# Prompt attention: the value products of a pair of heads side by side, block of keys by block, in a bank of their own

## The chip, the cores and the metric

The kernel runs on one core of one Trainium2 chip. The metric is the device time of one execution in microseconds (us). Engines: PE is TensorE (matrix products and transposes), DVE is VectorE, ACT is ScalarE, POOL is GpSimd (here mostly an issuer of DMAs), SP is SyncE (issues the weight loads). Every engine works through its own instructions in the order in which the built program has them, and waits on semaphores for the others.

## The reference, cut to what matters

One step of a decoder layer for a prompt of 512 tokens and 8 samples of 4 tokens. The part that is changed is the prompt's dilated attention: 12 heads of 64 columns, softmax over the keys allowed by three dilations, then the product with the values.

```python
HEAD_DIM = 64
DIL_HEADS = 12
DIL_PAIRS = ((128, 1), (512, 4), (2048, 16))
...
    s = jnp.einsum('bthd,btnhd->bthn', q, kg, preferred_element_type=jnp.float32) * (HEAD_DIM ** -0.5)
    s = jnp.where(valid[None, :, None, :], s, -jnp.inf)
    m = jnp.max(s, axis=-1, keepdims=True)
    p = jnp.exp(s - m)
    den = jnp.sum(p, axis=-1, keepdims=True)
    num = jnp.einsum('bthn,btnhd->bthd', p, vg.astype(jnp.float32))
```

Around it in the same layer: one input projection (for queries, keys, values, gates), a gated linear attention, an output projection, a convolutional feed-forward block and norms. The samples' attention over a cache of 1024 positions is computed beside the prompt's.

## The kernel before

Activations lie feature-major: 128 features on the partitions, 512 prompt and 32 sample tokens along the free axis. All big products are made in tiles of 128 output features (`in_tile`, L225): 16 blocks of input features, three products of split operands, two halves of 272 columns, so 96 matmuls to a tile, into one of two PSUM buffers `g`. A tile's result is taken out by DVE or ACT (`rope`, `scaled`, `gates`) into one of a few SBUF buffers, and only then is its PSUM buffer free for the tile after next.

The attention stage starts after six query tiles. For each of six pairs of heads it makes a key tile and a value tile, transposes the values (L584), and calls `prompt_attention`. That takes four blocks of 128 queries (`qi`), n = 128, 256, 384 and 512 keys, and in each the two heads (`e`): scores on PE (L548), bias and row maximum on DVE (L551, L553), exponential and row sum on ACT (L554), reciprocal on DVE (L555), scaling on ACT (L556), transposes of the probabilities on PE (L558), copy out of PSUM on ACT (L559), products with the values on PE (L561), copy of the result on ACT (L563). Scores, transposes and value products of one head and block share one PSUM tile `s`; there are three of these (`sps`), also used by the short transposes L382 and L584. A head's probabilities `t` come from five buffers (`ttile`). A value product has 128 rows and 64 columns of the array: head 0 writes partitions 0 to 63, head 1 partitions 64 to 127. Products of float32 operands show up in the trace as two instructions each (240 for the 120 of L561), transposes as one.

In the same stage run the samples' scores (`sample_scores`, DVE, with its loads issued by POOL) and, twice, `sample_mix`: softmax of the samples' scores (DVE L454 to L460, ACT L450, L464, L465, small PE transposes L444, L477, L484, L489) and their value products (L507), with cache blocks `kv` loaded by POOL (L395, L396) into four buffers that are freed by the products of the group before.

The order on each engine is found at build time by a scheduler that plays the program through on a timeline of its own; a tile's buffer is taken when its turn in the program's order of allocations comes. Weight loads and splits run ahead under a high priority. Two gates matter below. The evacuation of a projection tile needs a free SBUF buffer, which a pair of heads holds until its last scores are computed. And the gate tiles that come after the last pair need space which opens only when all prompt attention is done (`gates(DP)`, DVE L533).

Of the kernel before, what the change touches and what calls it, by code (L numbers as in the profile page):

```python
# [12 lines left out]
AF = mybir.ActivationFunctionType  # L13
# [4 lines left out]
P = 128  # L18
# [105 lines left out]
def _build(tc, nc, es, xT, st_gla, ck, cv, conv_in, vecs, w_in, w_gu, w_out, w_up, w_dn,  # L124
# [112 lines left out]
    def ttile(name, dt=F32):  # L237
        return PA.tile([P, NT], dt, tag="T", name=name, bufs=5)
# [61 lines left out]
    def sps():  # L300
        return pS.tile([P, 512], F32, tag="s", name="s")
# [4 lines left out]
    def in_tile(c0, units=None):  # L306
        ps = gps()
        gemm(ps, units or [wunit(w_in, ks, c0) for ks in H8], xg)
        return ps[:, :, :HT]
# [29 lines left out]
    for k in range(KD):  # L339
        for s in range(2):  # L340
            nc.tensor.matmul(psz[s][:2 * RANK, :HT], wz[:, k, :], xg[k][0][:, s * HT:(s + 1) * HT],
                             start=(k == 0), stop=False, skip_group_check=True)
            nc.tensor.matmul(psz[s][:RANK, :HT], wz[:, k, :RANK], xg[k][1][:, s * HT:(s + 1) * HT],
                             start=False, stop=(k == KD - 1), skip_group_check=True)
# [22 lines left out]
    def scaled(ps, name, mul=None):  # L367
        with evac():
            out = etile(name)
            if mul is None:  # L370
                nc.vector.tensor_mul(hv(out), ps, hv(rstd))
            else:
                nc.vector.scalar_tensor_tensor(hv(out), ps, mul, hv(rstd), op0=OP.mult, op1=OP.mult)
        return out
# [10 lines left out]
    o = [None] * KD  # L385
# [153 lines left out]
    def prompt_attention(p, q, k, vt):  # L539
        for e in range(2):  # L540
            r = slice(64 * e, 64 * e + 64)
            nc.scalar.activation(qz[r, e, :], q[r, :TP], AF.Copy)
        for qi in range(4):
            n = (qi + 1) * P
            for e in range(2):
                r = slice(64 * e, 64 * e + 64)
                psc = sps()
                nc.tensor.matmul(psc[:, :n], qz[:, e, qi * P:(qi + 1) * P], k[:, :n], start=True, stop=True)  # L548
                t = ttile("t")
                st = PA.tile([P, 4], F32, tag="st", name="st", bufs=6)  # L550
                nc.vector.tensor_tensor_reduce(t[:, :n], psc[:, :n], bp[:, (3 - qi) * P:], 0.125, -3e38,  # L551
                                               OP.add, OP.max, st[:, 0:1])
                nc.vector.tensor_scalar(st[:, 1:2], st[:, 0:1], -1.0, None, op0=OP.mult)  # L553
                nc.scalar.activation(t[:, :n], t[:, :n], AF.Exp, bias=st[:, 1:2], accum_out=st[:, 2:3])  # L554
                nc.vector.reciprocal(st[:, 3:4], st[:, 2:3])  # L555
                nc.scalar.activation(t[:, :n], t[:, :n], AF.Copy, scale=st[:, 3:4])  # L556
                for j in range(qi + 1):
                    nc.tensor.transpose(psc[:, j * P:(j + 1) * P], t[:, j * P:(j + 1) * P], ident)  # L558
                nc.scalar.activation(t[:, :n], psc[:, :n], AF.Copy)  # L559
                for j in range(qi + 1):  # L560
                    nc.tensor.matmul(psc[r, :P], vt[:, j * P + 64 * e:j * P + 64 * e + 64], t[:, j * P:(j + 1) * P],  # L561
                                     start=(j == 0), stop=(j == qi))
                nc.scalar.activation(o[10 + p][r, qi * P:(qi + 1) * P], psc[r, :P], AF.Copy)  # L563

    for p in range(DP):
        o[10 + p] = rowsA.tile([P, NT], F32, tag="R", name="ob")
# [8 lines left out]
    for p in range(DP):  # L575
        kT = rope(in_tile(C_KB + p * P), etile("rp"))
        vT = scaled(in_tile(C_VB + p * P), "vT")
        nc.scalar.dma_start(kT_p[p * P:(p + 1) * P, :], kT[:, :TP])
        nc.scalar.dma_start(vT_p[p * P:(p + 1) * P, :], vT[:, :TP])
        tok_s(kst[:, p * P:(p + 1) * P], kT)  # L580
        tok_s(vst[:, p * P:(p + 1) * P], vT)
        pst = sps()
        for j in range(4):
            nc.tensor.transpose(pst[:, j * P:(j + 1) * P], vT[:, j * P:(j + 1) * P], ident)  # L584
        vt = ttile("vt")
        nc.scalar.activation(vt[:, :TP], pst, AF.Copy)
        prompt_attention(p, o[10 + p], kT, vt)
        gates(p)
        if p == 3:
            sample_mix(0)  # L590
# [219 lines left out]
    for h in range(GATES_FIRST, 2 * GP):  # L810
        r = scaled(in_tile(C_RA + h * P), "r", -1.0)
# [92 lines left out]
    for ot in range(KD):  # L904
        ps = gps()
        gemm(ps, [wpart(w_out, order[:8], ot * P), wpart(w_out, order[8:], ot * P)], og)
        i, j = divmod(ot, 2)
# [384 lines left out]
```

## Time and profile before

| | us |
|---|---|
| median of 3 runs (lowest to highest) | 2537.07 (2533.39 to 2542.32) |
| the profiled execution | 2534.95 |
| its span | 2533.2 |
| PE busy in the span | 2460.0 (97%) |
| ACT busy | 1074.7 (42%) |
| DVE busy | 1626.6 (64%) |

The profiled execution is one run of the same program; the span leaves out 1.75 us of it. "Busy" on PE is modelled: a matmul's listed duration overlaps with the next one's, so what an instruction costs is read from starts, not from durations. The prompt attention lies between 130 and 426 us.

### The profile page before, as it was taken

Reading aid. Unit: us, or ns where it says so; the run is one execution under the profiler, and the core shown is the slowest. Engines: PE = TensorE matmul, PEld = TensorE weight load, DVE = VectorE, ACT = ScalarE, POOL = GpSimd, SP = SyncE. Lnnn points to the kernel's source line nnn. Section 1 sums busy time; section 2 is a strip of 40 time slices with the busy share of each in tenths; the row PEclk is TensorE's granted clock in tenths of the full one; section 3 lists DMA queues with packets and bytes.
Section 4 is the critical chain, followed back from the end, with each engine's and each line's share of the span. In section 5 each row is a group of like instructions: output and inputs, shape, how many; then the busy total and the mean of one; then the engine's idle time right before and its main releaser. Section 6 shows DMA issues by size and latency. Waiting matters only on the chain.

```text
span 2533.2 us, 47126 instructions
## 1 busy us (share of the span) xinstructions
PE 2460.0 (97%) x19479; PEld 2381.3 (94%) x19479; DVE 1626.6 (64%) x2432; ACT 1074.7 (42%) x1852; POOL 460.4 (18%) x593
## 2 busy tenths in 40 slices
PE   7999999999999999899999999999999999999997
PEld 7988987899999999899999999999999999999997
DVE  7778754277778853577787777777888643342244
ACT  5344554133334543454554455454555531231142
POOL 4343333300002400112222121222121000000001
PEclk9999999999999999899999999999999999999999
DMA  6777734532222363489999999999988473352332
GB/s 203 203 200 206 201 105 130 169 85 77 68 76 77 122 173 111 112 210 248 260 261 241 271 240 272 243 269 254 240 191 177 124 219 111 109 158 84 92 92 71
DMA packets 581593, 427.73 MB, mean 169 GB/s; under 512 B 18977, under 2 KB 553729, under 8 KB 580609
## 3 DMA queue, kind: packets, MB, share of 16 engines
q1 hardware_dynamic: 462144, 248.31, 35.3%
q0 software_dynamic: 115200, 171.02, 29.4%
q10 hardware_dynamic: 4032, 5.38, 0.6%
q8 instruction: 153, 2.51, 0.4%
q14 instruction: 64, 0.52, 0.1%
HBM read 397.40 MB, written 77.37 MB: 187 GB/s over the span
## 4 chain that ended last, share of the span: by engine, by line
PE 73%; DMA 15%; DVE 5%; issue 2%; ACT 2%; POOL 0%; DVEq 0%; SPq 0%; ACTq 0%; POOLq 0%
PE g L225 42%; PE b L939 14%; DMA raw<-in_w_up_dram 9%; PE g L939 9%; DMA q<-qscr 4%; DMA ar<-adr 1%; PE s L666 1%; PE v L507 1%; DVE wlo L191 1%; PE s L561 1%; ACT whi L190 1%; PE s L548 1%; DVE pr L411 1%; DVE h L1223 0%; PE s L558 0%
## 5 line engine op out<-in xcount | busy, mean ns | idle before, releaser
L190 ACT ACTIVATE whi<-raw 128x1024 fp32r<-128x1024 f32 (+1 forms) x345 | 355.2, 1030 | 622.3 <-PE g L225 459.8
L191 DVE TENSOR_TENSOR wlo<-raw,whi 128x1024 fp32r<-128x1024 f32 (+1 forms) x341 | 411.1, 1206 | 292.7 <-ACT whi L190 277.6
L225 PE MATMUL g<-ah,whi 128*128 128x272 f32 x2048 | 441.1, 294 | 3.3 <-ACT whi L190 2.1
L225 PE MATMUL g<-ah,wlo 128*128 128x272 f32 x2048 | 444.1, 294 | 0.0
L225 PE MATMUL g<-al,whi 128*128 128x272 f32 x2048 | 440.0, 294 | 0.0
L939 PE MATMUL b<-vh,whi 128*128 128x272 f32 x1376 | 398.5, 291 | 16.3 <-ACT whi L190 15.5
L939 PE MATMUL b<-vl,whi 128*128 128x272 f32 x1376 | 397.6, 290 | 0.0
L939 PE MATMUL b<-vh,wlo 128*128 128x272 f32 x1376 | 391.1, 289 | 0.0
L225 PEld LDWEIGHTS g<-ah,whi 128*128 128x128 f32 x2048 | 325.9, 189 | 14.9 <-issue 9.1
L225 PEld LDWEIGHTS g<-ah,wlo 128*128 128x128 f32 x2048 | 326.8, 189 | 8.3 <-issue 6.6
L225 PEld LDWEIGHTS g<-al,whi 128*128 128x128 f32 x2048 | 325.8, 190 | 8.2 <-issue 7.4
L939 PE MATMUL g<-vh,whi 128*128 128x272 f32 x1032 | 298.3, 289 | 3.2 <-ACT vh L883 3.2
L939 PE MATMUL g<-vl,whi 128*128 128x272 f32 x1032 | 299.0, 290 | 1.3 <-DVE vl L884 1.3
L939 PE MATMUL g<-vh,wlo 128*128 128x272 f32 x1032 | 296.7, 287 | 0.0
L939 PEld LDWEIGHTS b<-vh,whi 128*128 128x128 f32 x1376 | 261.2, 190 | 19.8 <-ACT whi L190 18.5
L225 PE MATMUL g<-dh,whi 128*128 128x272 f32 x1248 | 257.8, 288 | 4.5 <-ACT whi L190 2.6
L939 PEld LDWEIGHTS b<-vl,whi 128*128 128x128 f32 x1376 | 260.8, 190 | 0.0
L939 PEld LDWEIGHTS b<-vh,wlo 128*128 128x128 f32 x1376 | 258.7, 190 | 0.0
L225 PE MATMUL g<-dh,wlo 128*128 128x272 f32 x1248 | 257.4, 287 | 0.0
L225 PE MATMUL g<-dl,whi 128*128 128x272 f32 x1248 | 257.4, 288 | 0.0
L190 ACT ACTIVATE whi<-rs 128x1024 fp32r<-128x1024 f32 x129 | 136.6, 1059 | 257.9 <-PE g L939 159.3
L225 PEld LDWEIGHTS g<-dh,whi 128*128 128x128 f32 x1248 | 195.1, 188 | 6.1 <-ACT whi L190 3.2
(344 smaller groups left out, 4126.8 us busy)
## 6 DMA issues: line engine op xcount, KB each, us to landing
raw<-in_w_up_dram SPq DMA_DIRECT2D x129, 512.0 KB, 7.4
raw<-in_w_in_dram SPq DMA_DIRECT2D x96, 512.0 KB, 4.1
raw<-in_w_dn_dram SPq DMA_DIRECT2D x64, 512.0 KB, 4.0
out_k_s_dram<-in_ck_dram POOLq DMA_DIRECT2D x8, 3060.0 KB, 16.5
out_v_s_dram<-in_cv_dram POOLq DMA_DIRECT2D x8, 3060.0 KB, 16.8
ra<-in_w_up_dram SPq DMA_DIRECT2D x43, 512.0 KB, 7.1
rs<-in_w_up_dram SPq DMA_DIRECT2D x43, 512.0 KB, 3.8
rs<-in_w_up_dram POOLq DMA_DIRECT2D x43, 512.0 KB, 10.7
```

Source lines behind the costliest of these rows:

```text
L190: nc.scalar.activation(hi, src, AF.Copy)
L191: eng.tensor_sub(lo, src, hi.bitcast(F32))
L225: nc.tensor.matmul(ps[:, s, :HT], a, b[:, s * HT:(s + 1) * HT], start=(i == 0 and n == 0), stop=(i == len(todo) - 1 and n == 2))
L411: nc.vector.tensor_mul(pr, kt[:, 4:5, :].broadcast_to([P, TS, QC]), q5[:, 1:5, :])
L507: nc.tensor.matmul(psv[32 * m:32 * m + 32, :QC], lhs, rhs, start=(kt == 0), stop=(kt == 5), tile_position=(0, 32 * m))
L548: nc.tensor.matmul(psc[:, :n], qz[:, e, qi * P:(qi + 1) * P], k[:, :n], start=True, stop=True)
L561: nc.tensor.matmul(psc[r, :P], vt[:, j * P + 64 * e:j * P + 64 * e + 64], t[:, j * P:(j + 1) * P], start=(j == 0), stop=(j == qi))
L666: nc.tensor.matmul(ps[:, c * P:(c + 1) * P], KS[:, c * P:(c + 1) * P], Q[:, :, c * 64:(c + 1) * 64], start=True, stop=True)
L939: nc.tensor.matmul(b[:, :HT], a_[:, i, :], x_[i][:, v, :], start=(first and i == 0 and n == 0), stop=(i == 7 and n == 2), skip_group_check ...
```

## The change

The two heads of a block of queries no longer finish one after the other. Each head still makes its scores, softmax and transposes in a PSUM tile of its own. Its probabilities are kept in a list, and when both are there, a third PSUM tile `po` takes the value products: for each block of keys first head 0's, then head 1's, into the two halves of its partitions. One copy of 128 x 128 takes the place of two of 64 x 128. The line numbers after the change are 3 higher from L564 on (L561 becomes L564, L563 becomes L566, L584 becomes L587).

```diff
         for qi in range(4):
             n = (qi + 1) * P
+            ts = []
             for e in range(2):
-                r = slice(64 * e, 64 * e + 64)
                 psc = sps()
...
                 nc.scalar.activation(t[:, :n], psc[:, :n], AF.Copy)
-                for j in range(qi + 1):
-                    nc.tensor.matmul(psc[r, :P], vt[:, j * P + 64 * e:j * P + 64 * e + 64], t[:, j * P:(j + 1) * P],
-                                     start=(j == 0), stop=(j == qi))
-                nc.scalar.activation(o[10 + p][r, qi * P:(qi + 1) * P], psc[r, :P], AF.Copy)
+                ts.append(t)
+            po = sps()
+            for j in range(qi + 1):
+                for e in range(2):
+                    nc.tensor.matmul(po[64 * e:64 * e + 64, :P], vt[:, j * P + 64 * e:j * P + 64 * e + 64],
+                                     ts[e][:, j * P:(j + 1) * P], start=(j == 0), stop=(j == qi), skip_group_check=True)
+            nc.scalar.activation(o[10 + p][:, qi * P:(qi + 1) * P], po[:, :P], AF.Copy)
```

The scheduler lays the whole attention stage out anew. Three places show it.

The first is PE at the end of the 20th projection tile (`g_3917`, the values of the last pair). Before, the next tile (`g_4180`) follows at once, with the scores of pair 4 (`s_3548`) laid in between:

```order
L225 MATMUL g_3917<-ah15_202,wlo_3927 128x272 x2
L225 MATMUL g_4180<-ah0_106,whi_4183 128x272 x2
L225 MATMUL g_4180<-al0_107,whi_4183 128x272 x2
L225 MATMUL g_4180<-ah0_106,wlo_4184 128x272 x2
L225 MATMUL g_4180<-ah1_112,whi_4183 128x272 x2
L225 MATMUL g_4180<-al1_113,whi_4183 128x272 x2
L548 MATMUL s_3548<-rp_3411,qz_443 128x128
```

Now the attention of pair 3 stands there (`s_2795` to `s_2899`; `s_2817` and `s_2845` are the new banks `po`), without a row of L225:

```order
L225 MATMUL g_3917<-ah15_202,wlo_3927 128x272 x2
L558 MATMUL s_2795<-small_73,t_2797 128x128
L558 MATMUL s_2806<-small_73,t_2808 128x128
L564 MATMUL s_2817<-t_2797,vt_2791 64x128
L548 MATMUL s_2821<-rp_2658,qz_443 128x256
L564 MATMUL s_2817<-t_2808,vt_2791 64x128
L548 MATMUL s_2833<-rp_2658,qz_443 128x256
L477 MATMUL v_3108<-small_73,p0_3068 128x48 x4
L558 MATMUL s_2821<-small_73,t_2823 128x128 x2
L484 MATMUL v_3114<-small_73,p1_3069 128x48 x4
L558 MATMUL s_2833<-small_73,t_2835 128x128 x2
L564 MATMUL s_2845<-t_2823,vt_2791 64x128
```

It goes on so through the scores of the fourth block of queries; the tile `g_4180` begins behind them. At this count of projection tiles pair 3 has all its probabilities before the change, and only its first block's now.

The second place is PE at the end of the 23rd projection tile. Before, these rows stand there, where the last pair is at its third and fourth block:

```order
L516 MATMUL v_3291<-small_73,oT_3126 128x128 x3
L558 MATMUL s_4118<-small_73,t_4120 128x128 x3
L561 MATMUL s_4086<-t_4088,vt_4041 64x128 x2
L561 MATMUL s_4101<-t_4103,vt_4041 64x128 x3
L561 MATMUL s_4118<-t_4120,vt_4041 64x128 x3
L548 MATMUL s_4135<-rp_3908,qz_443 128x512
```

Now the whole attention of the last pair stands behind that tile, all four blocks, and with it the start of the second `sample_mix`. Of its third block (`s_4127` is `po`) the rows are:

```order
L564 MATMUL s_4127<-t_4103,vt_4041 64x128
L548 MATMUL s_4135<-rp_3908,qz_443 128x512
L507 MATMUL v_4518<-vst_440,pn__4483 32x192 x4
L558 MATMUL s_4114<-small_73,t_4116 128x128 x3
L507 MATMUL v_4559<-kv_4547,pe__4481 32x192
L564 MATMUL s_4127<-t_4116,vt_4041 64x128
L564 MATMUL s_4127<-t_4103,vt_4041 64x128
L564 MATMUL s_4127<-t_4116,vt_4041 64x128
L564 MATMUL s_4127<-t_4103,vt_4041 64x128
L564 MATMUL s_4127<-t_4116,vt_4041 64x128
L548 MATMUL s_4149<-rp_3908,qz_443 128x512
```

A block's products come in two pieces: head 0's first alone, and the rest when head 1 is ready; scores of the next block stand behind each piece. Between the pieces is a product that needs a freshly loaded block of the cache (`kv_4547`).

The third is ACT in the fourth block of the last pair. Before, the two heads' steps alternate:

```order
L554 ACTIVATE t_4137,st_4138<-t_4137,st_4138 128x512
L450 ACTIVATE p0_4447<-v_4450 48x512
L554 ACTIVATE t_4156,st_4157<-t_4156,st_4157 128x512
L556 ACTIVATE t_4137<-t_4137,st_4138 128x512
L450 ACTIVATE p1_4448<-v_4456 48x4x128
L556 ACTIVATE t_4156<-t_4156,st_4157 128x512
L559 ACTIVATE t_4137<-s_4135 128x512
```

Now the copy of the third block's result (`s_4127`) stands between head 0's exponential and its scaling, and head 1's steps come after all of head 0's:

```order
L554 ACTIVATE t_4137,st_4138<-t_4137,st_4138 128x512
L566 ACTIVATE ob_952<-s_4127 128x128
L556 ACTIVATE t_4137<-t_4137,st_4138 128x512
L559 ACTIVATE t_4137<-s_4135 128x512
L554 ACTIVATE t_4151,st_4152<-t_4151,st_4152 128x512
L556 ACTIVATE t_4151<-t_4151,st_4152 128x512
L559 ACTIVATE t_4151<-s_4149 128x512
```

From the feed-forward block on the order on all engines is as before.

## Rows read from the trace of the kernel before

**Rows 1.** The page: busy time of the span, and PE in 40 slices.
```profile
PE 2460.0 (97%) x19479; PEld 2381.3 (94%) x19479; DVE 1626.6 (64%) x2432; ACT 1074.7 (42%) x1852; POOL 460.4 (18%) x593
...
PE   7999999999999999899999999999999999999997
```

**Rows 2.** Groups of PE and ACT instructions by shape, 130 us on: busy, mean ns, idle before.
```profile
L561 PE MATMUL s<-t,vt 128*64 128x128 f32 x240 | 33.4, 283 | 0.0
...
L563 ACT ACTIVATE ob<-s 64x128 f32<-64x128 f32 x48 | 13.0, 271 | 35.9 <-PE s L561 35.4
```

**Rows 3.** Timeline of PE, a lone product of one head: start, us, line, count.
```profile
147.50 0.41 PE L225 MATMUL g<-ah,whi 128*128 128x272 f32 x2
147.84 0.43 PE L561 MATMUL s<-t,vt 128*64 128x128 f32 x2
148.20 0.39 PE L225 MATMUL g<-al,whi 128*128 128x272 f32 x1
```

**Rows 4.** Timeline of PE, four products of one head.
```profile
238.05 0.41 PE L225 MATMUL g<-ah,wlo 128*128 128x272 f32 x2
238.39 1.09 PE L561 MATMUL s<-t,vt 128*64 128x128 f32 x8
239.41 0.39 PE L225 MATMUL g<-ah,whi 128*128 128x272 f32 x1
```

**Rows 5.** Timeline of PE, six products that alternate between the two column halves.
```profile
616.10 0.41 PE L225 MATMUL g<-ah,whi 128*128 128x272 f32 x2
616.35 0.41 PE L225 MATMUL g<-al,whi 128*128 128x272 f32 x2
616.69 0.88 PE L721 MATMUL s<-V,kt 128*64 128x128 f32 x12
617.50 0.39 PE L225 MATMUL g<-ah,wlo 128*128 128x272 f32 x1
```

**Rows 6.** Stretches: us, busy of PE, PEld, DVE, ACT, POOL, granted clock, DMA, GB/s.
```profile
229.80:232.20 2.40, 0.13 (x2) 0.00 (x0) 2.40 (x5) 1.12 (x3) 0.33 (x1) 0.99 0.95 287
232.20:235.60 3.40, 2.74 (x13) 2.74 (x14) 2.44 (x6) 3.04 (x8) 1.77 (x3) 0.51 0.59 164
413.10:425.70 12.60, 9.15 (x67) 6.12 (x65) 7.77 (x19) 9.87 (x27) 4.83 (x10) 1.00 0.69 198
```

**Rows 7.** Timeline of all engines at the end of the attention stage.
```profile
409.71 0.91 PE L548 MATMUL s<-rp,qz 128*128 128x384 f32 x2
...
414.20 0.49 ACT L559 ACTIVATE t<-s 128x384 f32<-128x384 f32 x1 [0.35 <-PE s L558]
...
415.54 1.12 PE L548 MATMUL s<-rp,qz 128*128 128x512 f32 x2
...
416.70 0.69 DVE L551 CUSTOM_DVE_ANT_0 t<-s,bp 128x512 f32<-128x512 f32 x1 [1.89 <-PE s L548]
...
418.04 0.72 ACT L554 ACTIVATE t<-t,st 128x512 f32<-128x512 f32 x1
...
420.08 0.71 ACT L556 ACTIVATE t<-t,st 128x512 f32<-128x512 f32 x1
...
422.52 1.91 PE L561 MATMUL s<-t,vt 128*64 128x128 f32 x16
...
424.93 0.71 DVE L533 SCALAR_TENSOR_TENSOR oa<-g,rstd 128x544 f32<-128x544 f32 x1
...
425.70 0.52 PE L225 MATMUL g<-ah,whi 128*128 128x272 f32 x2 [1.27 <-DVE oa L533]
```

**Rows 8.** Groups of DVE instructions by shape, 405 to 428 us (samples' softmax).
```profile
L454 DVE TENSOR_REDUCE stt<-p 48x4 f32<-48x512 f32 x2 | 2.1, 1072 | 0.5 <-ACT p L450 0.5
...
L460 DVE TENSOR_TENSOR p<-p,stt 48x640 f32<-48x640 f32 x1 | 0.8, 809 | 0.0
```

**Rows 9.** POOL's timeline where a cache block is reloaded, and the median us to landing.
```profile
460.19 0.55 POOL L395 DMA_DIRECT2D kv<-in_cv_dram  x1 [10.89 <-PE v L507]
...
kv<-in_cv_dram POOLq DMA_DIRECT2D x32, 96.0 KB, 4.6
```

## The prediction

> **What bounds the kernel now.** First the page: PE is busy 97% of the span, in every slice but the first in nines or eights [rows 1]. So PE's queue is the path, and a microsecond of PE work or of PE waiting taken out of, or put into, the attention stage comes out of, or goes into, the end. Then the groups by shape: the value products L561 are 240 instructions, and the copies L563 are 48 at 271 ns on ACT, before which ACT sat idle 35.4 us waiting for those products [rows 2]; ACT has time. Third, the timeline of PE around three kinds of product runs, since listed durations overlap and only starts give a price. Last, the stretches in which PE did wait: the end of the stage at 413 us, where the span of 12.60 us has 9.15 us of listed PE work, and a wait at 229.8 us [rows 6].
>
> **The price of a value product.** Two L225 matmuls start every 0.25 us, 0.125 each [rows 5]. A lone product (two instructions) pushes the next L225 from 147.75 (147.50 + 2 x 0.125) to 148.20: 0.45 us [rows 3]. Four products of one head push it from 238.30 to 239.41: 1.11 us [rows 4]. So a run costs 0.24 for going into the half-width form and out of it, and 0.109 for each instruction. Six products that alternate between the halves push from 616.60 to 617.50: 0.90 us [rows 5], which is 0.24 + 6 x 0.109: instructions in different halves run two at a time, and only the busier half counts.
>
> Before, a pair with every head in a run of its own pays 2 x (0.45 + 0.67 + 0.89 + 1.11) = 6.24 us, six pairs 37.4. The order has 41 runs instead of 48, seven of them with pieces of both heads; at 0.24 and some overlap each I take off 4: 33.4.
>
> After, if the products of a block stood in one run, the busier half would have 2, 4, 6 and 8 instructions: 0.46 + 0.68 + 0.90 + 1.12 = 3.16, six pairs 19.0, a gain of 14.4. But the order puts head 0's first product alone (0.45) in 23 of 24 blocks, and the rest in a second run whose busier half is head 1's: 0.45, 0.68, 0.90, 1.12. That is 4.95 a pair, 29.7 in all, less 0.5 for the one block in one piece: 29.2. **Term 1: 4 us less on PE** (0 to 14 less, for other mergings).
>
> The Trainium skill (TensorEngine Tiling (Array Packing), Tiling Modes) says that tiles operate independently and a half-width form gives up to twice the rate. By that alone half of 33.4 goes, and the sum would be 17 less. Rows 5 agree with it for alternating instructions; the order here alternates only within the second piece.
>
> 24 copies of 271 ns go from ACT, 6.5 us. I cost that at nothing: ACT's idle time there is larger than that, and where ACT is on the path below, a copy of the block still stands in it.
>
> **What the order opens.** Before, a head keeps one PSUM tile from scores to result, so three heads are under way independently. Now a block takes three tiles in turn, and the next block's first scores stand behind the block's first value product. Two heads advance in step, and four steps make a pair. The attention slips behind the projection tiles: at the end of tile 20 it is a pair late. PE then has two stretches without a projection matmul.
>
> The length of a step is read from the end of the stage [rows 7]. At n = 512 head 0's scores start at 415.54 and its value product at 422.52: 7.0 us, with the maximum at 416.70, the exponential at 418.04 and the scaling at 420.08. At n = 384 one head takes from 409.71 to the end of its copy at 414.69: 5.0. For 256 and 128 I take 4.5 and 3.5, an estimate from the 5.0 with less to do; both lie between 3 and 5.0.
>
> *Stretch A, after tile 20 (pair 3).* The order on ACT puts two exponentials of the samples' softmax and a weight split ahead of the copies of the first block: 3.5 us. Step 256: 4.5 and 1.5 for the samples' reductions that DVE has ahead of it (1.07 and 0.81 are two of them [rows 8]). Step 384: 5.0 and 0.5. Then the last scores, a maximum (0.69) and the evacuation (0.7) that frees the projection's PSUM: 2.3. Together 17.3. The PE work in it (three value blocks in pieces 4.0, scores 2.1, transposes 0.8, samples' products and transposes 1.7) is 8.5. **Term 2: 9 us of waiting** (0 to 13). At 0 it would be covered by projection matmuls, and none is in the order there.
>
> *Stretch B, after tile 23 (pair 5).* Its start, with the last pair's transposed values and first scores: 2.5. Step 128: 3.5, and 2.5 for the samples' work that stands ahead on DVE. Step 256: 4.5 and 2. Step 384: 5.0. Then PE comes to a samples' product that needs a cache block which POOL can load only when the group before has been used; the issue takes 0.55 and the landing 4.6 [rows 9], 5.2 in all. Head 1's transposes, which end about 1.7 after that release, are just ahead of it, so PE stands 3.5, and behind it stand head 1's value products, the last scores, and on ACT the copy that now precedes head 0's scaling. Step 512: 7.0. Head 1's steps run after head 0's on ACT: scaling, transposes, copy and 1.1 of products more, then the evacuation of 0.71 [rows 7]: 3. Sum 33.5. PE work in it: value products 5.0 and 1.1 of pair 4, scores 2.4, transposes 1.9, samples' products 3 and small transposes 1: about 14. Waiting 19.5. The stretch that it replaces is 12.6 long [rows 6], with about 7.5 of work by the prices above: 5 of waiting. **Term 3: 14.5 more** (3 to 21: at the low end steps of 384 cost as much as 256 and the cache block is there, at the high end each step is 7.0).
>
> *Elsewhere.* Pairs 0 to 2 have about as many projection matmuls between scores and transposes as before, and the short waits of pairs 3 to 5 of before lie in the stretches now: **term 4: 2 less** (6 less to 4 more). After a wait of 2.40 us in which PE did 0.13 the granted clock was 0.51 for 3.40 us, the lower of the two levels [rows 6]; that costs some 1.7 where projection matmuls run. The two stretches have waits longer than that one in them. **Term 5: 3 more** (0 to 7). Behind the stage nothing is left to hide: PE there is full in both, and the feed-forward order is the same.
>
> Sum: -4 + 9 + 14.5 - 2 + 3 = +20.5. Against the profiled execution (2534.95) that is 2555.5; the median of the runs shown is 2.1 above it, so 2557 in round numbers.
>
> **The rivals.** *The packing wins* (6%): the steps are short enough, in the chip's times, to leave A and B as tight as 413 us was, and the products pair up: -14 to -4. For it speaks that six alternating products cost 0.90. Against it: the pieces are fixed in the order. It decides if A and B together hold under 10 us of waiting beyond the 5. Time 2537 - 14 + 2 = 2525. Half rate everywhere, by the rule quoted above, would be 2520.
>
> *No change that can be told* (10%): A waits 3, B 8: -4 + 3 + 3 - 2 + 2 = +2, 2539. For it: a scheduler's order that looks empty of projection rows can still be full, as the stretch at 413 us with its 9.15 of 12.60 listed. Against it: four dependent steps cannot be shorter than the sum of their parts in rows 7.
>
> *Low clock and stalls that follow* (14%): in stretches that are half idle the clock stays at 0.5, so scores and products in the chain double (about 10 us of PE work on the chain in A and B), and the samples' second group, now packed into fewer projection matmuls, waits for its cache blocks: another 10 to 25. 2570 to 2585. For it: the 0.51 of rows 6; against it: no drop at 413 us, where the clock was 1.00.
>
> *The forecast* (70%): 2545 to 2570.
>
> **How the numbers follow.** About 0.3% (7.6 us) is what a measurement of this kernel can tell from no change: 2529 to 2545. Slower takes the forecast and the heavy case, and loses a little at the forecast's lower edge: 0.84. Within: 0.10. Faster: 0.06. The low end, 2541, leaves out the packing and most of no change; the high end, 2577, half of the heavy case.
>
> **What would show it.** In the changed profile: value products of a block in two runs, the second about 0.45 to 1.1 for 2 to 14 instructions with starts in pairs; two gaps in the L225 rows, before tile 21 (17 us) and before tile 24 (33 us), with PE waiting for ACT's `t` and, in the second, a samples' product waiting for a DMA; the last L564 some 20 us later than the last L561 of before, which is over by 424.4 [rows 7]; the span from there to the end unchanged within 4. The prediction is wrong if those gaps are filled, if the gap in B is under 20, or if the time goes or comes after the attention stage.

## The result, and the profile after

The changed kernel is slower: 2560.22 us, median of 4 runs (2557.05 to 2565.06), against 2539.70 (2533.39 to 2542.67, 4 runs) for the kernel before, a ratio of 1.0086 with a 95% interval of 1.0063 to 1.0109. That is 20.5 us more, 16 to 28 by the interval. The profiled execution took 2565.06, the slowest of the four; its span is 30.1 us longer than the one of before, of which some 10 are the distance of these two runs from their medians. In the three later sets the kernel before took 2533.2 to 2534.0, 6 us less than beside the changed kernel, so the size of the loss is known to some 6 us only. One execution of the first experiment's kernel took 9661.81 us, and the time and the ratio given there leave it out.

In the changed kernel the lines from L564 on are those of before plus 3 (value products L561 are L564, the copy L563 is L566). The page, beside [rows 1]: more busy time on PE, and eights for nines in the third and the seventh slice (128 to 192 and 384 to 448 us). The sum hides more than it shows, so the place has to be found otherwise.

```profile
PE 2473.6 (96%) x19479; PEld 2383.3 (93%) x19479; DVE 1627.9 (64%) x2432; ACT 1069.0 (42%) x1828; POOL 456.0 (18%) x593
...
PE   7989998999999999999999999999999999999997
```

Where the time goes is read by counting L225 matmuls, which are the same 10272 in both programs, and looking when a given one starts:

| L225 matmul | before | after | difference |
|---|---|---|---|
| last of tile 20 (the 1920th) | 341.3 | 330.3 | -11 |
| first of tile 21 | 341.4 | 353.7 | +12 |
| last of tile 23 | 413.1 | 416.9 | +4 |
| first of tile 24 (the 2209th) | 425.7 | 455.0 | +29 |
| 4609th | 854.4 | 881.2 | +27 |
| 6144th | 1050.6 | 1075.7 | +25 |
| end of the span | 2533.2 | 2563.3 | +30 |

So the loss is made in two places, ahead of tile 21 and ahead of tile 24, and the stretches between run ahead, since attention work has left them. Both places, and the parts of them at the lower clock, as stretches of the profile (columns as in [rows 6]: us, busy of PE, PEld, DVE, ACT, POOL, granted clock, DMA, GB/s):

```profile
330.80:353.70 22.90, 18.96 (x110) 9.21 (x109) 10.19 (x32) 11.59 (x30) 5.08 (x8) 0.70 0.22 55
417.00:455.10 38.10, 29.44 (x180) 15.68 (x177) 18.66 (x53) 18.30 (x48) 7.97 (x11) 0.71 0.24 71
334.40:348.10 13.70, 11.62 (x69) 6.07 (x70) 4.83 (x18) 6.56 (x18) 0.00 (x0) 0.51 0.11 34
423.20:440.20 17.00, 14.74 (x65) 7.43 (x69) 9.26 (x28) 8.80 (x25) 0.00 (x0) 0.50 0.07 22
450.50:457.30 6.80, 5.98 (x37) 4.58 (x37) 1.36 (x2) 3.14 (x6) 0.00 (x0) 0.51 0.16 49
```

The reader is to see that no engine is busy throughout, and that PE ran 37.5 us in and just behind them at 0.5 of its clock, the lower of its two levels, 1.2 GHz. Before, the stage had 3.4 us of that [rows 6] (the changed kernel has such a piece too, at 184 us), and the stretch at 413 us, which the one ahead of tile 24 replaces, had none. The timeline of PE ahead of tile 21 shows what it did before the clock fell (start us, us, instruction, count, and in brackets the idle time before it with what ended that):

```profile
332.32 0.43 PE L564 MATMUL s<-t,vt 128*64 128x128 f32 x2 [1.46 <-ACT t L559]
332.68 0.70 PE L548 MATMUL s<-rp,qz 128*128 128x256 f32 x2
...
335.85 0.63 PE L477 MATMUL v<-small,p 48*128 48x48 f32 x4 [1.48 <-DVE p L459]
337.11 0.69 PE L558 MATMUL s<-small,t 128*128 128x128 f32 x2 [0.63 <-ACT t L556]
...
339.55 1.65 PE L548 MATMUL s<-rp,qz 128*128 128x384 f32 x2
...
353.66 0.52 PE L225 MATMUL g<-ah,whi 128*128 128x272 f32 x2 [0.37 <-DVE rp L362]
```

PE had waited 1.46 us and worked 1.92 when the clock halved at 334.24, just ahead of the second wait; after that one, of 1.48 us, the 384-key score product takes 1.65 us where it took 0.91 [rows 7]. It is on the chain: the maximum on DVE starts when that product ends (first row below). The rows under it are PE ahead of tile 24, where the clock fell at 422.99, inside the second of these waits. No single wait of PE in the two stretches is longer than 1.97 us.

```profile
341.24 0.56 DVE L551 CUSTOM_DVE_ANT_0 t<-s,bp 128x384 f32<-128x384 f32 x1 [3.76 <-PE s L548]
...
421.90 0.29 PE L444 MATMUL v<-small,s_x 32*48 32x32 f32 x4 [1.97 <-DVE s_x L434]
423.54 0.47 PE L558 MATMUL s<-small,t 128*128 128x128 f32 x1 [1.34 <-ACT t L556]
...
449.82 0.51 PE L507 MATMUL v<-kv,pe__4481 128*32 128x192 f32 x2 [1.60 <-DMA kv<-in_cv_dram]
...
452.12 1.97 PE L564 MATMUL s<-t,vt 128*64 128x128 f32 x14 [0.75 <-ACT t L559]
```

Then the groups by shape from 130 us on, to set beside [rows 2]; the same scores took 9.7 (384 keys) and 7.3 us (256 keys) before:

```profile
L564 PE MATMUL s<-t,vt 128*64 128x128 f32 x240 | 31.0, 307 | 3.2 <-ACT t L559 3.2
L558 PE MATMUL s<-small,t 128*128 128x128 f32 x120 | 24.4, 307 | 10.3 <-ACT t L556 10.2
...
L548 PE MATMUL s<-rp,qz 128*128 128x384 f32 x24 | 13.6, 664 | 0.0
L548 PE MATMUL s<-rp,qz 128*128 128x256 f32 x24 | 9.4, 478 | 0.0
```

What the lower clock costs in such a stretch can be read where the same order ran with more and with less of it. The kernels at the end of the next section that have only three or five of the gated part's seven levels keep their partner's order in the attention stage. First the stretch at 413 us in before's order, with three levels and with five (12.60 us with all, at 1.00 [rows 6]); then the stretch ahead of tile 21 in the changed order, with five and with three (22.90 with all):

```profile
412.10:425.30 13.20, 10.15 (x66) 6.96 (x64) 7.78 (x18) 9.52 (x27) 4.74 (x9) 0.87 0.64 189
412.60:426.50 13.90, 11.05 (x67) 7.57 (x65) 7.81 (x19) 9.94 (x27) 4.77 (x9) 0.77 0.61 180
```
```profile
328.60:349.60 21.00, 16.88 (x109) 8.30 (x108) 10.06 (x32) 11.40 (x30) 5.01 (x8) 0.84 0.23 60
327.00:347.70 20.70, 16.56 (x109) 8.34 (x109) 10.05 (x32) 11.39 (x30) 5.07 (x8) 0.84 0.23 63
```

By the granted clock the first two hold 3.4 and 6.4 us at the lower level where before has none, and the other two 6.7 where the changed kernel has 13.7. So a microsecond at the lower level lengthened such a stretch by 0.2 to 0.3 us. Ahead of tile 24 the changed order shows less: 36.9 and 38.1 us with 17 and 21 at the lower level, against 38.1 with 22.

### The profile page after: what moved, and what is told of

It reads as the page before. It is cut to its first block, busy times and chain, and to the rows that moved or that the text cites. A ratio compares the mean times of both kernels' runs of the same rounds, so it can differ in the third digit from the quotient of the medians.

```text
span 2563.3 us, 47095 instructions
## 1 busy us (share of the span) xinstructions
PE 2473.6 (96%) x19479; PEld 2383.3 (93%) x19479; DVE 1627.9 (64%) x2432; ACT 1069.0 (42%) x1828; POOL 456.0 (18%) x593
## 3 DMA queue, kind: packets, MB, share of 16 engines
q0 software_dynamic: 115200, 171.02, 29.2%
## 4 chain that ended last, share of the span: by engine, by line
PE 73%; DMA 13%; DVE 7%; issue 2%; ACT 1%; POOL 0%; DVEq 0%; ACTq 0%; SPq 0%; POOLq 0%
PE g L225 40%; PE b L942 16%; PE g L942 11%; DMA raw<-in_w_up_dram 7%; DMA q<-qscr 5%; DMA ar<-adr 1%; PE v L507 1%; DVE pr L411 1%; DVE wlo L191 1%; PE s L669 1%; PE s L548 1%; ACT whi L190 1%; PE s L564 1%; DVE h L1226 0%; DVE kv L412 0%
## 5 line engine op out<-in xcount | busy, mean ns | idle before, releaser
L225 PE MATMUL g<-ah,whi 128*128 128x272 f32 x2048 | 442.6, 294 | 2.6 <-ACT whi L190 2.1
L225 PE MATMUL g<-al,whi 128*128 128x272 f32 x2048 | 439.5, 294 | 1.0 <-DVE al L191 1.0
L225 PE MATMUL g<-ah,wlo 128*128 128x272 f32 x2048 | 437.3, 293 | 0.0
L942 PE MATMUL b<-vh,whi 128*128 128x272 f32 x1376 | 399.2, 291 | 19.4 <-ACT whi L190 18.6
L225 PEld LDWEIGHTS g<-ah,whi 128*128 128x128 f32 x2048 | 326.7, 190 | 13.3 <-issue 8.4
L225 PEld LDWEIGHTS g<-al,whi 128*128 128x128 f32 x2048 | 326.5, 190 | 8.0 <-issue 5.2
L225 PEld LDWEIGHTS g<-ah,wlo 128*128 128x128 f32 x2048 | 325.9, 189 | 4.6 <-issue 3.1
L225 PE MATMUL g<-dh,whi 128*128 128x272 f32 x1248 | 257.6, 288 | 4.1 <-ACT whi L190 2.1
L225 PE MATMUL g<-dl,whi 128*128 128x272 f32 x1248 | 257.6, 288 | 0.0
L225 PE MATMUL g<-dh,wlo 128*128 128x272 f32 x1248 | 257.5, 287 | 0.0
L942 PEld LDWEIGHTS g<-vh,whi 128*128 128x128 f32 x1032 | 195.7, 190 | 6.9 <-ACT vh L886 6.9
```

The source lines that it names most:

```text
L225: nc.tensor.matmul(ps[:, s, :HT], a, b[:, s * HT:(s + 1) * HT], start=(i == 0 and n == 0), stop=(i == len(todo) - 1 and n == 2))
L942: nc.tensor.matmul(b[:, :HT], a_[:, i, :], x_[i][:, v, :], start=(first and i == 0 and n == 0), stop=(i == 7 and n == 2), skip_group_check ...
```

## The experiments

Theory T: the block's third tile, not the pairing, opens the two stretches. Rival W: it is that both heads must be ready before the products. Rival P: the order of the products within the block matters. The first four kernels were run together; the kernel before took 2533.98 us beside them (19 runs).

**A tile of its own, heads not paired.**

```diff
+                po = sps()
                 for j in range(qi + 1):
-                    nc.tensor.matmul(psc[r, :P], ...
+                    nc.tensor.matmul(po[r, :P], ...
-                nc.scalar.activation(o[10 + p][r, ...], psc[r, :P], AF.Copy)
+                nc.scalar.activation(o[10 + p][r, ...], po[r, :P], AF.Copy)
```

> The kernel before with one thing added: each head's value product goes into a PSUM tile of its own instead of back into the tile of its scores; the heads stay unpaired. Theory T (the third PSUM tile taken in turn is what slows the stage): its order has three stretches without projection matmuls, before tiles 18, 21 and 24, of 48, 130 and 202 rows, so it is slower than before by more than the change is, 2570 to 2620 us, with the granted clock near 0.5 in parts of them. Rival W (waiting for both heads before either's value product is what slows it): nothing waits for both heads here, so 2540 us, as before.

Measured: 2685.53 us (three executions), ratio 1.0598 (1.0569 to 1.0627). The direction is T's and W falls, but T's size was far too small. Stretches without a projection matmul stand behind 1632, 1920 and 2208 of them; the two last took 71 and 98 us, at a granted clock of 0.63 and 0.64 (columns as above):

```profile
382.90:453.80 70.90, 46.13 (x218) 23.84 (x216) 13.18 (x47) 29.10 (x71) 11.32 (x20) 0.63 0.27 81
498.20:596.40 98.20, 63.56 (x347) 32.53 (x346) 26.72 (x79) 34.34 (x82) 21.14 (x29) 0.64 0.23 68
```

**Paired, each head in its old tile.** As the change, but `po` is each head's own score tile, and each is copied out by itself.

```diff
+                ps2.append(psc)
-            po = sps()
+                    nc.tensor.matmul(ps2[e][64 * e:64 * e + 64, :P], ...
```

> The pairing without the third tile: products of the two heads alternate as in the change, but each goes into the tile of its head's own scores, with two copies of 64 partitions. Theory T: its order has one stretch, before tile 24 (77 rows, between the 45 of before and the 111 of the change), 45 product runs: 2530 to 2550 us. Rival W: both heads are waited for, so as slow as the change, 2555 to 2565 us.

Measured: 2540.19 us, ratio 1.0018 (1.0004 to 1.0032). As T expected; W falls: waiting for both heads costs 1 to 8 us by the interval. Nor does pairing bring anything here: the order has the products in 45 runs, and they are listed with 33.3 us, as before [rows 2].

**Paired, both heads in the second head's score tile.**

```diff
-            po = sps()
+            po = ps2[1]
```

> The change with one edit: the shared bank is head 1's score tile, free once its transposes are copied out, instead of a third tile. Theory T: two tiles for a block, and the order has every block's products in one run (24 runs) and no long stretch without projection matmuls, so the whole saving of about 14 us on PE shows and the 5 us of waiting at the end of the stage mostly goes: 2515 to 2530 us. Rival W: head 0 waits for head 1 even longer here, 2555 us or more.

Measured: 2537.91 us, ratio 1.0014 (1.0002 to 1.0025). W falls again, but T's number (2515 to 2530) missed too: the saving of about 14 us on PE is not in the time. It is in the trace. The products stand in 24 runs, one a block. First their group from 130 us on (the value products are L565 here), then the page's line of busy times, PE 15.3 us under [rows 1]:

```profile
L565 PE MATMUL s<-t,vt 128*64 128x128 f32 x240 | 18.4, 283 | 0.9 <-ACT t L559 0.9
```
```profile
PE 2444.7 (96%) x19479; PEld 2371.1 (93%) x19479; DVE 1622.2 (64%) x2432; ACT 1064.7 (42%) x1828; POOL 462.6 (18%) x593
```

By matmul count this kernel is 11 us ahead at tile 24 and 15 at the 2593rd; at the 4801st, where before starts it at 882.0, it is 5 us behind. What PE waits for between 829.9 and 900 us (us in total, times, longest), and after it PE's timeline there:

```profile
PE g L225 <- ACT ah L190: 4.8, 1, 4.8
PE s L670 <- DVE ST L673: 4.2, 1, 4.2
PE g L225 <- DVE h L916: 3.3, 1, 3.3
```
```profile
829.83 0.41 PE L225 MATMUL g<-ah,whi 128*128 128x272 f32 x2
834.47 2.05 PE L670 MATMUL s<-QB,KB 128*128 128x128 f32 x8 [4.23 <-DVE ST L673]
...
872.52 0.41 PE L776 MATMUL s<-sq,onesV 128*128 128x64 f32 x2 [1.12 <-DVE oa L781]
877.75 1.27 PE L225 MATMUL g<-ah,whi 128*128 128x272 f32 x4 [4.83 <-ACT ah L190]
...
886.88 0.60 PE L225 MATMUL g<-ah,whi 128*128 128x272 f32 x2 [3.32 <-DVE h L916]
```

PE waits for the gated linear attention, on which VectorE works nearly all the time (39.62 of the 40 us from 800): first at a product of its levels (L670), then, when at 867 us no projection matmul is left that doesn't need its result, at its end. That part starts when the samples' attention has finished, and the samples' values come in groups of four cache blocks, each group loaded when the one before has been used. In twelve of the thirteen traces of this document its first product starts 36 to 38 us after the last of these loads is issued (61 in the first experiment's kernel). That load on POOL's timeline, first of the changed kernel, then of this one:

```profile
481.35 0.61 POOL L395 DMA_DIRECT2D kv<-in_cv_dram  x1
```
```profile
484.49 0.61 POOL L395 DMA_DIRECT2D kv<-in_cv_dram  x1
```

In before it is issued at 481.6, and the first product of the gated levels starts at 518.5, 518.2 and 522.5 us (before, after, this one). So in these three kernels PE's stream may be 25 us slower or 15 faster, and the start of this second chain hardly moves. In the order of before its last normalizing product stands behind 4688 of the 4776 projection matmuls that can cover it; here behind all 4776. The end of the chain in before, the split of its last result on ACT, and the first projection matmul that takes it up:

```profile
871.95 1.30 ACT L190 ACTIVATE ah<-oa 128x544 fp32r<-128x544 f32 x2 [3.30 <-DVE oa L813]
```
```profile
878.95 0.41 PE L225 MATMUL g<-ah,whi 128*128 128x272 f32 x2
```

Two pieces end by 873.25, so PE could have come some 6 us sooner and no more. Here PE comes at 867 and goes on at 877.75; from 872.9 to 887.0 its granted clock is 0.64, and the 5 us behind at the 4801st are these waits and that clock together. This is theory B: two chains of almost equal length, so that a loss on PE counts and a gain doesn't.

**The change with the heads in turn.**

```diff
-            for j in range(qi + 1):
-                for e in range(2):
+            for e in range(2):
+                for j in range(qi + 1):
```

> The change without the alternation: in the shared third tile first all of head 0's products, then all of head 1's. Theory T: the order has the same two stretches (73 and 89 rows instead of 67 and 111), the products cost about 4 us more on PE than in the change, so 2555 to 2570 us, within 0.4% of the change. Rival P (the price of the products decides): back to the product price of before and more, slower than the change by 10 us or more.

Measured: 2562.98 us, ratio 1.0114 (1.0094 to 1.0133). The time is in T's range. Against the changed kernel it is 2.8 us more by the medians and 7 more by the two ratios, with 0 to 15 left open by their intervals, and the products are listed with 36.9 us against 31.0. So alternating is worth a few us here; P's 10 or more isn't seen, but not ruled out.

**The gated part on five of seven levels** (these kernels leave out the two finest), in three kernels that were run together with the next (2533.20 us for before, 17 runs), to take the second chain out of the way.

```diff
-        for n, h in enumerate(LEVELS):
+        for n, h in enumerate(LEVELS[:5]):
```

> The kernel before, with the gated part's loop over seven levels cut to the first five (the two finest, h = 2 and 1, are left out, so this part of the output isn't the reference's). It is the partner of the next two kernels. Theory B (two chains of nearly equal length end together: the TensorE stream, and beside it the chain of sample values and gated part, which VectorE and the cache loads pace): the second chain gets some 45 us shorter, TensorE loses only the work of the two levels, 80 + 20 instructions of about 0.13 us, 13 us: 2516 to 2526 us. Rival S (TensorE's stream alone sets the time in the kernel before and in the paired ones): the same, 2516 to 2526 us.

> Products paired in the second head's own score tile, as in the third kernel of the first set, and the gated part on five levels of seven (its output isn't the reference's there). Theory B: with the second chain out of the way, the 15 us that pairing takes out of TensorE's stream come through: 12 to 18 us under the partner with five levels, 2500 to 2514 us. Rival S (the 15 us are lost in TensorE's own stream, to waits or to the lower clock, whatever stands beside it): within 5 us of the partner.

> The changed kernel with the gated part on five levels of seven (its output isn't the reference's there). Theory B: in the changed kernel TensorE's stream is the longer chain by some 25 us, so that nothing is hidden by the second one: 20 to 30 us over the partner with five levels, 2538 to 2556 us. Rival S: the same as between the full kernels, 20 us, which lies in that range too; under 12 us over the partner would speak against both, since then the gated part itself made a share of the loss.

Measured: 2521.25, 2512.76 and 2536.23 us, ratios to before of 0.9950 (0.9935 to 0.9966), 0.9913 (0.9881 to 0.9944) and 1.0010 (0.9997 to 1.0023). The first is as expected by both theories. The second is 8.5 us under its partner, where it had been 4 over with all levels: B's direction, under B's 12 to 18, and with these intervals not sure against S. The third, 15 us over its partner, lies in neither range. By matmul count the stage itself lost as much as expected (23.7 us at tile 24), and 10 of it came back by the 4609th.

**The pair's tile from the samples' bank.**

```diff
-            po = sps()
+            po = vps()
```

> The changed kernel with the pair's own tile taken from the single v bank, which the sample part's products use, and not from the three s banks. Its order has one stretch without a gemm in place of two: 121 instructions behind tile 23, none behind tile 20. Theory T (the time goes in stretches of attention work in a row, each of which waits at every softmax, whichever pool made them): after's two stretches of 67 and 111 instructions took 23 + 38 us, 0.34 us an instruction, and the kernel with a tile per head took 0.57; so 41 to 69 us here against 12.6 us before, less 0.15 us for each of the 76 instructions that come out of the interleaved part: 17 to 45 us slower than the kernel before, 2550 to 2580 us. Rival N (only the shortage of the three s banks costs, a fourth tile from elsewhere is free): 2520 to 2540 us.

Measured: 2562.38 us, ratio 1.0110 (1.0084 to 1.0137). In T's range, and N falls, but less than half of the loss has T's reason. The stretch behind tile 23 took 47.9 us (0.40 an instruction); the tiles ahead of it ran 23 us early, so that tile 24 starts 13 us late and the 2593rd matmul 8.5. The other 20 are lost at the gated part's end, as in the kernel with the second head's tile: its last normalizing product, too, stands behind all 4776, and PE waits 4.8 and 4.2 us for the same two tiles. Here the second chain itself is late: the samples' last cache block is loaded 27 us later than before, and the first product of the gated levels starts at 546.3.

```profile
508.35 0.61 POOL L395 DMA_DIRECT2D kv<-in_cv_dram  x1
```

**The gated part on three levels**, three kernels run together in five rounds (2533.19 us for before, 17 runs), since with three levels all three orders keep over 400 matmuls behind the last normalizing product.

```diff
-        for n, h in enumerate(LEVELS):
+        for n, h in enumerate(LEVELS[:3]):
```

> The kernel before with the gated part on three levels of seven (h = 64, 32 and 16 alone; its output isn't the reference's there): the partner of the next two. Another 13 us of TensorE work less than with five levels: 2502 to 2514 us by both theories. In its order the last normalizing product of the gated part stands after 4304 of the 4776 projection matmuls that precede the output projection; with five levels it stood after 4432, with seven after 4688.

> Products paired in the second head's own score tile, gated part on three levels (output not the reference's there). Its last normalizing product stands after 4352 of 4776 matmuls; with seven levels it stood after all 4776. Theory B (with seven levels the gated chain took the saving at its end): 8 to 16 us under the partner, as the 8.5 us with five levels. Rival S (the saving is lost in TensorE's own stream whatever the gated part does): within 5 us of the partner.

> The changed kernel with the gated part on three levels (output not the reference's there). Theory B, mended after the 15 us with five levels: the attention stage loses some 25 us, and the stretch behind it gives some 10 back as the samples' products have moved into it: 10 to 20 us over the partner. Rival G (the gated part, not the attention stage, makes the loss, and the loss shrinks with it: 20.5 us with seven levels, 15 with five): 5 to 10 us over the partner.

Measured: 2509.32, 2497.06 and 2527.50 us, ratios 0.9903 (0.9888 to 0.9919), 0.9856 (0.9839 to 0.9873) and 0.9981 (0.9968 to 0.9994). The pair in the second head's tile is 12.3 us under its partner, some 6 to 18 by the two intervals: B holds and S falls. Between the 4401st L225 and the 5501st it now takes 139.9 us, as its partner does, where with all levels it took 178.6 against 157.6. The changed kernel is 18.2 us over its partner: the loss is the attention stage's, and G falls.

No kernel that computes the whole layer was faster than the kernel before; more space for the samples' cache blocks, which might shorten the second chain, wasn't tried.

## Why the prediction was right, and where not

The time (2557 forecast, 2560.2 measured) and the sign came by the forecast way, with one term too small, one pair of terms split wrongly and one sentence wrong. That 20.5 us were forecast and 20.5 measured is luck in part: in the profiled pair the last value product ends 29.7 us later (454.1 against 424.4, 20 forecast) and the 6144th matmul starts 25 later. From that last product to the end the pair is alike to 0.4 us.

- **The price of a product** held. 0.24 us for a run and 0.109 for an instruction of the busier half give 19.0 us for six pairs in 24 runs; the kernel that has them so lists 18.4. The same 240 instructions, alternating in the program of both kernels, are listed with 33.3 us in 45 runs and with 18.4 in 24. The Trainium skill (TensorEngine Tiling (Array Packing), Tiling Modes) says that a change of the tiling mode drains TensorE, without a time for it; the traces agree that a run has a price of its own, 0.24 us by [rows 3] and [rows 4]. For the change 29.2 were forecast and 31.0 are listed, part of them at the lower clock. The 17 us less that the prediction gives for twice the rate everywhere count the 4 of term 1 again; 13 would be right.
- **Term 1 and term 4** held, as far as their sum can be read. Some 15 us of work were to move into the stretches (8.5, and 14 for 7.5), 4 to fall away and 2 elsewhere: 21 us less outside them. By the table the projection gains 10.9 ahead of tile 21 and 8.5 between 21 and 24, 19.4.
- **Terms 2 and 3** had the right places and order of steps, with lengths that were short by 5.6 and 4.6: 17.3 and 33.5 forecast, 22.9 and 38.1 measured. Their split into work and waiting was wrong: PE has no listed work in 3.9 and 8.7 us of them, where 9 and 19.5 of waiting were forecast, and the rest is listed work, most of it at the lower clock. The wait for cache blocks, 3.5 forecast, was 2.6.
- **Term 5 is the step that was mis-sized**: 3 us (0 to 7) for the clock, priced where projection matmuls run. The lower clock held for 37.5 us, nearly all in the chain itself, and it came without the longer waits that the term reckoned with: the longest was 1.97 us, against the 2.40 of [rows 6]. From [rows 2]'s window to the same one of after, scores are listed with 41.4 us for 34.3, transposes with 24.4 for 22.5; the two stretches are 10.2 us over their forecast. So term 5 and the stretches together are some 7 short. At 0.2 to 0.3 us for each of the 35 in the stretches, the price read above, the clock makes 7 to 11 us, an estimate that covers most or all of the 10; no run took the clock alone away. What spoke against the rival of the low clock, the 1.00 in the stretch at 413 us [rows 6], was one execution: the same stretch in the same order had 3.4 and 6.4 us of the lower level in the kernels with three and five levels.
- **"Behind the stage nothing is left to hide" failed.** It came out near enough for this change: tile 24 was 29 us late, the 6144th matmul 25. But PE at 97% was not the only path. The second chain's last product stands 88 matmuls, some 11 us, ahead of PE's need, and its last result is there some 6 us ahead; a PE stream made shorter runs into it. So the rival in which the packing wins would not have come to 2525 even with 24 runs: the kernel in which the packing does win 15 us of PE takes 2537.9.
- **No change that can be told** is out by the interval. **Low clock and stalls that follow** had the mechanism of the missing 7 us, and about its size (10 us of PE work on the chain); the stalls that it adds to it didn't come.

What stays open is why 4 to 10 us come back behind the stage in the changed kernel. The samples' products that have moved ahead of tile 24 are one reason that the trace offers; it wasn't tested by itself.

## What to carry to other kernels

Count PSUM tiles before pairing anything: a result that lies in the tile of one of its operands' stages cost 6 us at most (1.0014, 1.0002 to 1.0025), the same result in a tile of its own cost 20.5 us, and one for each head 152, because the program's order then has long dependent stretches with no independent matmuls between. Judge a saving on the busiest engine by what ends beside it: PE at 97% could gain only some 6 us before it met the other chain, and a cut of 15 us on PE showed in the time only when that chain was cut as well. And allow for TensorE's lower clock in a stretch of short dependent steps, scores and transposes in the chain included; one trace at the full clock doesn't show that the next will have it.

## What the runs showed of the hardware

Here products in the two 64-column halves of the array gained when they stood in one run: with 45 runs for 24 blocks nothing was gained, with 24 runs the listed time fell to 0.55. In the changed kernel the granted clock fell to its lower level in two stretches of short dependent steps whose waits were 1.97 us at most (at 334.24 us after a wait of 1.46 and 1.92 of work), and in the stretch at 413 us the same order of instructions had 0, 3.4 or 6.4 us of it from kernel to kernel. And a listed busy time misleads at the lower clock: the stretch from 334.40 us shows 11.62 busy of 13.70 us at 0.51, since the work itself is listed longer there, 1.65 us for 0.91 in the case of the 384-key scores.
